# The first head's values are loaded behind the scores of its first query tile

## The chip, the core and the metric

The kernel runs on one core of a Trainium2 chip. The core has a matrix engine (PE, with its own path for loading weights, PEld), a vector engine (DVE), an activation engine (ACT), a general engine (POOL) and a queue engine (SP) that here issues every DMA. Times are microseconds (us) on the device. The metric is the time of one execution; the time before is the median of three runs.

## The reference

One layer of a streaming encoder with two branches. It handles a prompt of 2048 new frames and a sample of 64 frames of running streams. All of it is float32 and the kernel must return eight tensors (two outputs, keys, values and retention states). In short:

```python
h = rmsnorm(x, norm_g) @ w_in                  # 1024 -> 6144 columns
qa, ka, va, za, qb, kb, vb, zb, ga, gb = split(h)
# branch A: 4 heads, each with two 64-wide halves c = 0, 1 of q and k, values 128 wide
s = einsum('bqhcd,bkhcd->bhcqk', q, k) * 64 ** -0.5 - slope * |q_pos - k_pos|
s = where(k_pos // 64 <= q_pos // 64, s, -inf)
p = softmax(s)
a = p[:, :, 0] - lam * p[:, :, 1]
out_a = einsum('bhqk,bkhe->bqhe', a, v)        # then a norm per head
# branch B: retention, chunks of 64, state carried from chunk to chunk
y = x + (sig(ga) * (out_a * silu(za) @ w_o_diff) + sig(gb) * (out_b * silu(zb) @ w_o_ret)) @ w_out
```

## The kernel before

**Splitting.** A float32 product is made of products of high and low parts: every operand `w` is split by a cast on ACT (`wh`) and a subtraction on DVE or POOL (`wl`), and PE does `wh*xh`, `wh*xl` and `wl*xh`. Keys, queries and values are kept in DRAM as two such parts (`kT`, `qT`, `vN`, each a list of two).

**Stages.** Three generators run side by side. `w_stream` makes the input projection: an opening part, blocks done directly (L1137 is the matmul line of those) or by one level of Strassen's scheme (L989), and last `quad` (L1544), which makes the remaining gate columns in seven passes with names `t2, b11, b21, t1, t3, t4, b22`; every pass forms sums of the inputs' blocks and has matmuls on L1564. Its results are added up by DVE on L1584; the fifth pass, `t3`, needs two such additions for each group of matmuls. `z_stream` does the attention of the sample, then that of the prompt (`attn_head`, by half of the prompt, head and query tile `p`), with retention and norms between, then prepares the output stage (`out_prep`). In it the output weights are loaded and split (`load_wo`, L2470 the cast on ACT, L2477 the subtraction on DVE, L2473 that on POOL) and the gated branch results are formed (L2615, L2626). `out_stream` makes the output products.

**One query tile of the prompt attention.** `qk_block` issues, for each of two blocks of 128 queries and both halves c, the score matmuls (L1878 and L1879: high and low parts of `q`) into a bank named `mm`, `s` or `tp`, and a DVE reduction on L1887 that adds the position table (`dnear`, `dfar`) and keeps the minimum. `softmax` exponentiates on ACT (L1918) and combines both halves. `at_pv` transposes the result on PE (L1990, bank `at`), splits it (cast `ath` on ACT, L2004; `atl` on DVE, L2006), and multiplies it with the values (L1968, L1969, L1970, bank `pv`); `a_e` is a small row of sums that L2015 adds. It does not begin until both score blocks are done and the values' load is issued:

```python
yield lambda: pair["n"] == 2 and hd["tv"] is not None
arows, vs = pair["rows"], hd["vs"]
yield max(pair["t"], hd["tv"])
```

**The loads.** `h_loader` runs `load_head` for each head: four K loads (per half of the prompt), then two V loads of 512 KB (`vN[0]`, `vN[1]`). For the first head of all (`self.far` is false) the loads of the first two query tiles and of the table `dfar` stand between K and V. `self.ntile` counts the query tiles whose scores are out; `h_loader` waits for 3 of them before the second head.

**What sets the order.** The order of every engine is written when the program is built. `loop` is a planner: it holds a list of generators with priorities, and keeps a model clock for PE, ACT, DVE, POOL and DMA (`self.pe` and so on). It always runs the first generator, by priority, whose wake time or condition is met. `P`, `A`, `V`, `G`, `ld` and `st` advance the clocks by modelled costs. So a change in when one condition is met can give another order to everything planned later. PE, ACT and DVE run the order as written; each waits at its next instruction until what that needs is done. All DMAs are issued by SP in order (`ld` on L280, `st` on L285) and go round eight semaphores (DMAHW0 to DMAHW7 in the lists below), so that each DMA's issue also waits until the eighth one before it has landed. Buffers that matter here: `thi` and `tlo` (parts of the values on their way to `vN`) have one and two, `ath` and `atl` two each, V four, q two; of PSUM banks there are two `mm`, two `s`, two `at`, one `pv`, one `tp`.

Of the kernel before, what the change touches and what calls it, by code (L numbers as in the profile page):

```python
# [172 lines left out]
class Hybrid:  # L173
# [1595 lines left out]
    def load_head(self, half, h):  # L1769
        ap = self.ap  # L1770
        nu = half + 1
        ks = [[None] * nu for _ in range(2)]
        vs = [[None] * nu for _ in range(2)]
        tk = tv = 0
        for u in range(nu):
            usl = slice(1024 * u, 1024 * u + 1024)
            for c in range(2):
                yield from self.take("K")
                k = self.sb(ap, [128, 1024], "K", dt=F32R)
                for j in range(2):  # L1780
                    o = 64 * (j ^ c)
                    tk = self.ld(k[o:o + 64].bitcast(F32), self.kT[j][h, 64 * c:64 * c + 64, usl], 1 << 18)
                ks[c][u] = k
        hd = {"ks": ks, "vs": vs, "tk": tk, "tv": None}
        if self.far:
            self.heads.append(hd)
        else:
            self.far = True
            yield from self.load_q(0, 0)
            yield self.pe + 3000  # L1790
            yield from self.load_q(0, 1)
            yield self.pe + 2000
            self.ld(self.dfar, self.i["c_dfar"], 1 << 19)
            self.heads.append(hd)
        for u in range(nu):
            usl = slice(1024 * u, 1024 * u + 1024)
            for j in range(2):
                yield from self.take("V")
                v = self.sb(ap, [128, 8, 128], "V", dt=F32R)
                tv = self.ld(v.bitcast(F32), self.vN[j][usl, 128 * h:128 * h + 128]  # L1800
                             .rearrange("(t p) e -> p t e", p=128), 1 << 19)
                vs[j][u] = v
        hd["tv"] = tv
# [1399 lines left out]
```

## Time and profile before

| what | value |
|---|---|
| median of three runs | 1887.12 us (1886.89 to 1887.62) |
| the profiled execution: its time, its span | 1887.63 us, 1885.9 us |
| PE, DVE, ACT, POOL busy | 99%, 71%, 52%, 36% of the span |
| granted PE clock | 1.00 |
| matmuls (PE), transfers on SP's queue | 11090 instructions, 61.7% of 16 DMA engines |
| prompt attention's first score matmul (L1878) | 604.5 us |
| `quad`, first to last addition on L1584 | 1454.8 to 1532.4 us |

The profile counts an engine as busy from an instruction's start to its modelled end. Matmuls overlap, so a matmul's cost on PE is the distance from its start to the next one's start. An entry `[1.31 <-DMA q<-qT]` says that the engine stood idle for 1.31 us before the instruction and that the load of `q` ended that.

### The profile page before, as it was taken

The numbers are of one execution on the slowest core, as the hardware profiler recorded it, in microseconds if no ns is written. First come the engines' busy times: TensorE is split into PE (matmuls) and PEld (weight loads), VectorE is DVE, ScalarE is ACT, GpSimd is POOL, SyncE is SP. The second block draws the span as 40 slices with busy tenths as digits, with TensorE's granted clock in tenths as the row PEclk, the third lists the DMA queues.
The fourth block names the chain that finished last, engine by engine and source line by source line (L and its number), as shares of the span: only waits on it lengthen the run. The fifth ranks groups of instructions, "written<-read, shape, count | busy, mean of one in ns | idle before, by whom it ended". The sixth has DMA issues, their size and how long they took to land.

```text
span 1885.9 us, 33029 instructions
## 1 busy us (share of the span) xinstructions
PE 1867.0 (99%) x11090; PEld 1644.9 (87%) x11090; DVE 1330.5 (71%) x3117; ACT 975.9 (52%) x2266; POOL 669.5 (36%) x723
## 2 busy tenths in 40 slices
PE   9999999999999999999999999999999999999999
PEld 7788878888888789888988889899999899998887
DVE  6765857658585677787587777677866969977664
ACT  6444545554434566556465655556666436654221
POOL 2420266555552122022210344243224625512442
PEclk9999999999999999999999999999999999999999
DMA  7664555666867967556423649446437988886452
GB/s 258 209 177 122 162 165 169 177 199 198 243 185 191 254 196 191 154 170 174 139 73 95 178 131 244 120 130 158 115 115 231 284 233 257 271 237 209 165 157 77
DMA packets 402555, 340.07 MB, mean 180 GB/s; under 512 B 85329, under 2 KB 348625, under 8 KB 401362
## 3 DMA queue, kind: packets, MB, share of 16 engines
q1 hardware_dynamic: 402386, 337.97, 61.7%
q8 instruction: 87, 1.43, 0.3%
q14 instruction: 82, 0.67, 0.1%
HBM read 218.27 MB, written 118.75 MB: 179 GB/s over the span
## 4 chain that ended last, share of the span: by engine, by line
PE 89%; DMA 4%; DVE 4%; issue 1%; SPq 1%; ACT 1%; POOL 0%; DVEq 0%; ACTq 0%; POOLq 0%
PE mm L1137 29%; PE mm L989 8%; PE tp L989 4%; PE at L1990 3%; PE s L1879 2%; PE s L1878 2%; PE s L989 2%; PE pv L1970 2%; PE pv L1969 2%; PE pv L1968 2%; PE mm L1564 1%; PE s L2793 1%; PE s L2795 1%; PE s L2794 1%; PE pv L2256 1%
## 5 line engine op out<-in xcount | busy, mean ns | idle before, releaser
L748 POOL TENSOR_TENSOR wl<-ws,wh 128x512 fp32r<-128x512 f32 x102 | 142.5, 1408 | 240.8 <-ACT wh L727 160.2
L1137 PE MATMUL mm<-wh,xh 128*128 128x512 f32 x504 | 203.0, 403 | 0.0
L1137 PE MATMUL mm<-wh,xl 128*128 128x512 f32 x504 | 198.1, 393 | 0.0
L1137 PE MATMUL mm<-wl,xh 128*128 128x512 f32 x504 | 198.0, 393 | 0.1
L1137 PE MATMUL mm<-xh,wh 128*128 128x288 f32 (+2 forms) x544 | 179.8, 330 | 0.0
L1137 PE MATMUL mm<-xh,wl 128*128 128x288 f32 (+2 forms) x544 | 175.5, 323 | 0.0
L1137 PE MATMUL mm<-xl,wh 128*128 128x288 f32 (+2 forms) x544 | 175.5, 323 | 0.0
L1918 ACT ACTIVATE row<-row,a_mx 128x1024 f32<-128x1024 f32 (+7 forms) x144 | 149.8, 1042 | 11.7 <-DVE a_mx L1897 11.7
L2006 DVE TENSOR_TENSOR atl<-at,ath 128x512 fp32r<-128x512 f32 (+1 forms) x144 | 92.6, 658 | 77.8 <-ACT ath L2004 77.6
L2004 ACT CAST ath<-at 128x512 fp32r<-128x512 f32 (+1 forms) x144 | 79.1, 564 | 106.2 <-PE at L1990 105.7
L856 POOL TENSOR_TENSOR wl<-ws,wh 128x256 fp32r<-128x256 f32 x64 | 55.3, 865 | 197.8 <-ACT wh L847 197.6
L1745 POOL TENSOR_TENSOR r_y<-r_y,r_sq 128x256 f32<-128x256 f32 x32 | 29.7, 929 | 236.2 <-DVE r_sq L1742 152.4
L1137 PEld LDWEIGHTS mm<-wh,xl 128*128 128x128 f32 x504 | 94.6, 188 | 21.6
L1137 PEld LDWEIGHTS mm<-wl,xh 128*128 128x128 f32 x504 | 95.0, 188 | 18.4 <-POOL wl L748 0.9
L1137 PEld LDWEIGHTS mm<-wh,xh 128*128 128x128 f32 x504 | 94.9, 188 | 17.8 <-DVE raw L1308 0.2
L1137 PEld LDWEIGHTS mm<-xh,wh 128*128 128x128 f32 x544 | 102.4, 188 | 7.2
L1137 PEld LDWEIGHTS mm<-xl,wh 128*128 128x128 f32 x544 | 102.5, 188 | 6.9
L1137 PEld LDWEIGHTS mm<-xh,wl 128*128 128x128 f32 x544 | 102.3, 188 | 6.6
L1887 DVE CUSTOM_DVE_ANT_0 row<-s,dfar 128x512 f32<-128x512 f32 (+2 forms) x141 | 87.0, 629 | 23.4 <-PE s L1879 16.8
L1940 DVE SCALAR_TENSOR_TENSOR row<-row,a_w 128x1024 f32<-128x1024 f32 (+5 forms) x88 | 97.3, 1111 | 0.0
L727 ACT CAST wh<-ws 128x512 fp32r<-128x512 f32 x111 | 67.7, 619 | 47.9 <-DMA ws<-wsum 13.2
L1878 PE MATMUL s<-K,q 128*128 128x512 f32 (+3 forms) x240 | 90.5, 379 | 1.3 <-DVE a_acc L1887 1.3
(543 smaller groups left out, 6072.4 us busy)
## 6 DMA issues: line engine op xcount, KB each, us to landing
ws<-in_w_in_dram SPq DMA_DIRECT2D x155, 256.0 KB, 3.4
q<-qT SPq DMA_DIRECT2D x128, 128.0 KB, 3.8
K<-kT SPq DMA_DIRECT2D x48, 256.0 KB, 4.6
V<-vN SPq DMA_DIRECT2D x24, 512.0 KB, 5.9
row<-in_x_prompt_dram SPq DMA_DIRECT2D x16, 512.0 KB, 4.5
wz<-in_w_in_dram SPq DMA_DIRECT2D x32, 256.0 KB, 4.3
row<-in_cache_k_T_dram SPq DMA_DIRECT2D x32, 256.0 KB, 3.2
row<-in_cache_v_diff_dram SPq DMA_DIRECT2D x32, 256.0 KB, 3.6
```

Of the source, the lines that this page charges most:

```text
L727: self.nc.scalar.copy(h, st)
L748: eng.tensor_sub(l, st, h.bitcast(F32))
L856: nc.gpsimd.tensor_sub(l[:, cs], src, h[:, cs].bitcast(F32))
L989: nc.tensor.matmul(ps, w[:, c], xs[x][c], start=bool(tag) and c == 0 and i == 0, stop=c == 3 and i == 2, skip_group_check=True)
L1137: nc.tensor.matmul(ps, p, q, start=c == 0 and i == 0, stop=c == KC - 1 and i == 2)
L1878: nc.tensor.matmul(ps, q1s, kk, start=True, stop=False)
L1887: nc.vector.tensor_tensor_reduce(out=row[:, k0:k0 + n], in0=ps, in1=tab, scale=-SLOPES[h], scalar=3.0e38, op0=ALU.add, op1=ALU.min, accum_ ...
L1918: nc.scalar.activation(u, u, AF.Exp, bias=mx, scale=-1.0, accum_out=lp[:, k:k + 1])
L1940: nc.vector.scalar_tensor_tensor(out=u0, in0=u1, scalar=w[:, 0:1], in1=u0, op0=ALU.mult, op1=ALU.add)
L1990: nc.tensor.transpose(at[:, w:w + 128], src, self.ident)
L2004: nc.scalar.copy(ah[:, :w], at[:, :w])
L2006: nc.vector.tensor_sub(al[:, :w], at[:, :w], ah[:, :w].bitcast(F32))
```

## The change

A condition is added to `load_head`, in the branch for the first head of all: after the table load and after the head has been put into the list, the generator waits until one query tile's scores are out, and only then issues the V loads.

```diff
             yield self.pe + 2000
             self.ld(self.dfar, self.i["c_dfar"], 1 << 19)
             self.heads.append(hd)
+            yield lambda: self.ntile >= 1
         for u in range(nu):
             usl = slice(1024 * u, 1024 * u + 1024)
             for j in range(2):
```

Lines behind L1794 are one higher in the changed kernel (L2005 there is L2004 here, L1969 is L1968, L2478 is L2477). The set of instructions is almost the same on every engine: 10790 rows on PE and 1544 on SP in both, and three subtractions of L748 (`wl` of an input weight) go from DVE to POOL. Their order differs from the moved loads on to the end of the attention and into `quad`.

**SP, at the first tile.** In the kernel before, behind the table:

```order
L280 DMA dfar<-in_c_dfar_dram 128x1920 [waits DMAHW4_49]
L280 DMA V<-vN_61 128x8x128 [waits DMAHW5_49]
L280 DMA V<-vN_62 128x8x128 [waits DMAHW6_49]
L285 DMA qbT<-ev 128x256 [waits DMAHW7_49,Activation_49]
L285 DMA gbT<-ev 128x2x256 [waits DMAHW0_49,DVE_49]
L285 DMA qbT<-ev 128x256 [waits DMAHW1_49,Activation_49]
L285 DMA qbT<-ev 128x32 [waits DMAHW2_49,Activation_49]
L285 DMA qbT<-ev 128x256 [waits DMAHW3_49]
L280 DMA q<-qT_57 64x2x256 [waits DMAHW4_49,PE_49]
L280 DMA q<-qT_57 64x2x256 [waits DMAHW5_49]
```

In the changed kernel:

```order
L280 DMA dfar<-in_c_dfar_dram 128x1920 [waits DMAHW4_49]
L285 DMA qbT<-ev 128x256 [waits DMAHW5_49,Activation_49]
L285 DMA gbT<-ev 128x2x256 [waits DMAHW6_49,DVE_49]
L285 DMA qbT<-ev 128x256 [waits DMAHW7_49,Activation_49]
L285 DMA qbT<-ev 128x32 [waits DMAHW0_49,Activation_49]
L285 DMA qbT<-ev 128x256 [waits DMAHW1_49]
L280 DMA V<-vN_61 128x8x128 [waits DMAHW2_49]
L280 DMA V<-vN_62 128x8x128 [waits DMAHW3_49]
L280 DMA q<-qT_57 64x2x256 [waits DMAHW4_49,PE_49]
L280 DMA q<-qT_57 64x2x256 [waits DMAHW5_49]
```

Both V loads go behind five stores (of `qbT` and `gbT`, results of the projection) and stand right ahead of the first load of the next `q`.

**PE, at the second tile's scores.** Before, where `tp`, `s` on L1878 and L1879 are the second tile's scores, `mm` on L1137 the projection, and `pv` the first tile's product with V:

```order
L1878 MATMUL tp<-K,q 128x256
L1879 MATMUL tp<-K,q 128x256
L1878 MATMUL s<-K,q 128x384
L1879 MATMUL s<-K,q 128x384
L1878 MATMUL s<-K,q 128x256
L1879 MATMUL s<-K,q 128x256
L1137 MATMUL mm<-wh,xh_120 128x512
L1137 MATMUL mm<-wl,xh_120 128x512
L1137 MATMUL mm<-wh,xl_121 128x512
L1968 MATMUL pv<-ath,V 128x256
L1969 MATMUL pv<-ath,V 128x256
L1970 MATMUL pv<-atl,V 128x256
```

Changed:

```order
L1137 MATMUL mm<-wh,xh_120 128x512
L1137 MATMUL mm<-wl,xh_120 128x512
L1137 MATMUL mm<-wh,xl_121 128x512
L1137 MATMUL mm<-wh,xh_120 128x512
L1137 MATMUL mm<-wl,xh_120 128x512
L1137 MATMUL mm<-wh,xl_121 128x512
L1969 MATMUL pv<-ath,V 128x256
L1970 MATMUL pv<-ath,V 128x256
L1971 MATMUL pv<-atl,V 128x256
L1969 MATMUL pv<-ath,V 128x128
L1970 MATMUL pv<-ath,V 128x128
L1971 MATMUL pv<-atl,V 128x128
```

The first tile's products with V now come behind six matmuls of the projection and ahead of the second tile's scores, which follow behind the `a_e` row and three more matmuls of the projection.

**ACT, some 25 us later.** `r_o`, `r_y`, `r_sq` and `r_hi` belong to the norms of retention and of the projection, `thi` and `raw` to values that are stored. Before:

```order
L1703 ACTIVATE r_sq<-r_o 128x256
L1705 ACTIVATE r_hi<-r_o 128x256
L2004 CAST ath<-at 128x512
L1384 CAST thi<-mm 128x512
L1386 COPY raw<-mm 128x512
L2004 CAST ath<-at 128x512
L1729 ACTIVATE r_y<-tp 128x256
L1730 ACTIVATE r_y<-r_y 128x256
L1731 ACTIVATE r_sq<-r_y 128x256
L2004 CAST ath<-at 128x384
```

Changed:

```order
L1703 ACTIVATE r_sq<-r_o 128x256
L1705 ACTIVATE r_hi<-r_o 128x256
L1384 CAST thi<-mm 128x512
L1386 COPY raw<-mm 128x512
L1729 ACTIVATE r_y<-tp 128x256
L1730 ACTIVATE r_y<-r_y 128x256
L1731 ACTIVATE r_sq<-r_y 128x256
L2005 CAST ath<-at 128x512 x2
L2005 CAST ath<-at 128x384
```

The first cast of `at` went behind `thi`, `raw` and the three norm steps, and the three casts of `at` now stand together.

**DVE, in the fifth pass of `quad`.** `u` and `ev` on L1584 are the additions that empty PSUM banks, `xl` the low part of a sum of inputs for a later pass, `w_o_diffl` and `w_o_retl` those of the output weights. Before:

```order
L2477 TENSOR_TENSOR w_o_retl_16953<-wst,w_o_reth_16952 128x2x256
L1584 TENSOR_TENSOR u_16726<-at,u_16726 128x256
L1584 TENSOR_TENSOR u_16727<-at,u_16727 128x288
L748 TENSOR_TENSOR wl<-ws,wh 128x512
L1584 TENSOR_TENSOR u_16726<-mm,u_16726 128x256
L2477 TENSOR_TENSOR w_o_diffl_16951<-wst,w_o_diffh_16950 128x2x256
L1584 TENSOR_TENSOR u_16727<-mm,u_16727 128x288
L2477 TENSOR_TENSOR w_o_retl_16955<-wst,w_o_reth_16954 128x2x256
L1584 TENSOR_TENSOR u_16726<-s,u_16726 128x256
L1584 TENSOR_TENSOR ev<-s,u_16726 128x256
L1584 TENSOR_TENSOR u_16727<-s,u_16727 128x288
L1584 TENSOR_TENSOR ev<-s,u_16727 128x288
```

Changed, at the same count of rows:

```order
L1584 TENSOR_TENSOR u_16576<-at,u_16576 128x288
L2478 TENSOR_TENSOR w_o_diffl_17152<-wst,w_o_diffh_17151 128x2x256
L1529 TENSOR_TENSOR xl_123<-xraw,xh_122 128x544
L1584 TENSOR_TENSOR u_16575<-at,u_16575 128x256
L1584 TENSOR_TENSOR ev<-at,u_16576 128x288
L2478 TENSOR_TENSOR w_o_retl_17154<-wst,w_o_reth_17153 128x2x256
L1529 TENSOR_TENSOR xl_123<-xraw,xh_122 128x544
L1584 TENSOR_TENSOR u_16576<-mm,u_16576 128x288
L2478 TENSOR_TENSOR w_o_retl_17156<-wst,w_o_reth_17155 128x2x256
L1584 TENSOR_TENSOR ev<-at,u_16575 128x256
L1584 TENSOR_TENSOR u_16575<-mm,u_16575 128x256
L2478 TENSOR_TENSOR w_o_diffl_17150<-wst,w_o_diffh_17149 128x2x256
```

The subtractions for the output weights came between additions in both; more of them, and more of `xl`, stand between the additions of this pass in the changed order.

## The prediction

> **What bounds the kernel now.** I read the page's head first, then the matrix engine's waits over the whole run, then its timeline at the places that the change touches, with the DMA queue's beside it, and last the stretches of `quad`.
>
> ```profile
> span 1885.9 us, 33029 instructions
> PE 1867.0 (99%) x11090; PEld 1644.9 (87%) x11090; DVE 1330.5 (71%) x3117; ACT 975.9 (52%) x2266; POOL 669.5 (36%) x723
> ```
>
> PE bounds the whole run, and the change neither adds nor takes a matmul. So it can only move the time by PE's waits: those it takes away, and those the new order makes. The waits put down to one cause, largest first:
>
> ```profile
> PE mm L1564 <- DVE ev L1584: 2.1, 1, 2.1
> ...
> PE s L1564 <- DVE xl L1529: 1.6, 1, 1.6
> PE tp L1878 <- DMA q<-qT: 1.3, 1, 1.3
> PE s L1878 <- DVE a_acc L1887: 1.3, 1, 1.3
> PE pv L1968 <- ACT ath L2004: 1.2, 1, 1.2
> ...
> PE s L1564 <- DVE u L1584: 0.9, 1, 0.9
> ```
>
> Three of these belong to `quad` (L1564), 4.6 us together; the others are single events in the attention.
>
> **The change, first tile: what it may remove.** The second tile's scores wait for their `q`:
>
> ```profile
> 615.96 0.29 PE L1137 MATMUL mm<-xl,wh 128*128 128x288 f32 x1
> 616.09 0.29 PE L1137 MATMUL mm<-xh,wl 128*128 128x288 f32 x1
> 617.68 0.36 PE L1878 MATMUL tp<-K,q 128*128 128x256 f32 x1 [1.31 <-DMA q<-qT]
> 618.39 0.36 PE L1879 MATMUL tp<-K,q 128*128 128x256 f32 x1 [0.35 <-DMA q<-qT]
> ...
> 619.18 0.40 PE L1137 MATMUL mm<-wh,xh 128*128 128x512 f32 x1
> 619.42 0.40 PE L1137 MATMUL mm<-wl,xh 128*128 128x512 f32 x1
> ...
> 619.88 0.28 PE L1968 MATMUL pv<-ath,V 128*128 128x256 f32 x1
> 620.00 0.28 PE L1969 MATMUL pv<-ath,V 128*128 128x256 f32 x1
> ...
> 620.66 0.42 PE L1878 MATMUL tp<-K,q 128*128 128x384 f32 x1
> ```
>
> From start to start a 128x288 matmul takes 0.13 us (616.09-615.96), a 128x512 one 0.24, a 128x256 one 0.12. The step from 616.09 took 1.59, 1.46 too long, that from 617.68 took 0.71, 0.59 too long: 2.05 us lost. In the new order six 128x512 matmuls come first (6 x 0.24, so PE wants V at 616.22+1.44 = 617.7), then the pv block with its a_e row (620.66-619.88 = 0.78) and three more 128x512 (0.72): PE wants the `q` at 619.2. Does the queue deliver both?
>
> ```profile
> 605.41 0.34 SPq L280 DMA_DIRECT2D dfar<-in_c_dfar_dram  x1
> 606.31 1.00 SPq L280 DMA_DIRECT2D V<-vN  x2
> 607.41 2.60 SPq L285 DMA_DIRECT2D qbT<-ev  x1
> 610.13 0.36 SPq L285 DMA_DIRECT2D gbT<-ev  x1
> 610.60 1.67 SPq L285 DMA_DIRECT2D qbT<-ev  x3
> 612.37 3.52 SPq L280 DMA_DIRECT2D q<-qT  x4
> ```
>
> The last of these q loads was issued before 615.9 and the stall ended at 618.4, so `q` is there by the new time if it is issued no more than 0.8 us later; V stands ahead of it, but V's issue (1.00) was ahead of it already. Two prices for V's issue: the five stores move up by V's 1.00 and the first of them, which took 2.60 right behind V, takes the 0.36 of the next one, so V goes out at 612.37-1.00-2.60+0.36 = 609.1; or the stores gain nothing, and V goes out at 612.4.
>
> ```profile
> DMA to landing us min/median/max: 5.6/6.3/6.9
> ...
> DMA to landing us min/median/max: 3.8/5.9/10.4
> ```
>
> The first row is V's in the stretch 600 to 616 us, the second all 24 V loads of the run. Issued at 609.1 V lands by 616.0, 1.7 ahead of 617.7. At the other end 612.4+6.9 = 619.3 is 1.6 late. So this term lies between -2.05 and -2.05+1.6 = -0.4. I take -2.05: the next store, from the same `ev` tiles but not right behind V, took 0.36.
>
> [...]
>
> **The second place: a wait that takes the place of the one removed.** Some 20 us later PE waits for casts of `at`:
>
> ```profile
> 640.99 0.38 PE L1968 MATMUL pv<-ath,V 128*128 128x256 f32 x1 [1.21 <-ACT ath L2004]
> ...
> 641.82 0.39 PE L1970 MATMUL pv<-atl,V 128*128 128x256 f32 x1 [0.33 <-DVE atl L2006]
> ```
>
> The cast that it waits for stands behind `thi`, and that behind the store of the last `thi` (one buffer):
>
> ```profile
> 639.37 0.58 ACT L1384 CAST thi<-mm 128x512 fp32r<-128x512 f32 x1 [2.78 <-DMA vN<-thi]
> ...
> 640.33 0.60 ACT L2004 CAST ath<-at 128x512 fp32r<-128x512 f32 x1
> 640.80 0.42 ACT L1729 ACTIVATE r_y<-tp 128x256 f32<-128x256 f32 x1
> ...
> 642.02 0.46 ACT L2004 CAST ath<-at 128x384 fp32r<-128x384 f32 x1
> ```
>
> ```profile
> 635.34 0.54 SPq L280 DMA_DIRECT2D ws<-in_w_in_dram  x1
> 635.98 0.41 SPq L285 DMA_DIRECT2D vN<-thi  x1
> ```
>
> In the new order `thi`, `raw`, `r_y`, `r_y` and `r_sq` all stand ahead of the casts. From `thi` to the cast was 0.96 (`thi` and `raw`); three norm steps add 1.22 (642.02-640.80). From the cast's start to PE's was 0.66. The `ws` issue in front of the store went ahead among the K loads, which lets the store out 0.64 earlier (635.98-635.34). So pv starts at 639.37-0.64+0.96+1.22+0.66 = 641.57, which is 0.58 later than before. By then PE has issued nine more 128x512 matmuls (9 x 0.24 = 2.16), three 128x128 transposes less (0.06 each, half of a 128x256) and six pv matmuls less (0.12 each): 1.23 us of work that is ahead. The balance of both places is 0.58-1.23 = -0.65; so this one costs +1.4 of the 2.05. Its bounds: all of the old wait gone (-1.21-0.33 = -1.5), or the store not earlier (+1.4+0.64 = +2.0).
>
> **The third place: the splits of the output weights fall into `quad`.** The planner ran more of the projection early, so fewer of its matmuls are left for later: by the order of the two kernels the last pv of the attention comes behind one group of `quad` before, behind twelve and a half now (828 and 690 matmuls of L1564 follow it). What waits for the end of the attention, above all the splits of the output weights on DVE, slides into the fifth pass, in which DVE has the most to do:
>
> ```profile
> 1482.00:1498.00 16.00, 14.04 (x108) 13.69 (x108) 16.00 (x24) 9.09 (x16) 13.86 (x9) 1.00 1.11 342
> 1498.00:1514.00 16.00, 13.95 (x109) 13.65 (x108) 14.94 (x26) 6.49 (x11) 9.92 (x7) 1.00 1.06 277
> ...
> L2477 DVE TENSOR_TENSOR w_o_diffl<-wst,w_o_diffh x5: 677/1435/1462, 1445.4 to 1489.0; 128x512 fp32r<-128x512 f32 x5
> ...
> L1529 DVE TENSOR_TENSOR xl<-xraw,xh x24: 707/1102/1854, 1425.3 to 1514.7; 128x544 fp32r<-128x544 f32 x24
> ...
> L2669 PE MATMUL s<-ogh,w_o_diffh x64: 279/283/289, 1532.2 to 1712.5; 128*128 128x264 f32 x64
> ```
>
> Columns of the first two rows: PE, PEld, DVE, ACT and POOL busy; of the others: shortest, median and longest in ns, first and last start. DVE is busy 16.00 of 16.00 us while PE is at 14.04: here DVE sets the pace, and each more row on it between additions delays PE. Counted in the two orders, between the 20th and 50th addition on L1584 stand 20 other rows before and 25 now (L1529 8 and 10, L2477 5 and 7, L2626 1 and 4, L748 3 and 1, L2615 3 each); between the 50th and 60th there are two fewer. Net three more rows at 1.10 us (the median of L1529, the commonest of them): +3.3. Bounds: nothing, if DVE's lead before this stretch takes them (five fewer stand between the 10th and 20th addition), or less than nothing if the waits of `quad` go (a rival below); above, all five at the 1.435 of L2477, +7.2.
>
> [...]
>
> What comes with it at no cost: three subtractions of L748 go from DVE to POOL (36% busy). The output weights come later by what the attention's end slides in PE's work, 138 matmuls x 0.13 = 18 us; the last DVE split started at 1489.0 and the first output matmul at 1532.2, so 43 us of cover hide it, and it would cost only beyond that. The store and load issues are the same number; nothing else on SP waits for V.
>
> **The sum.** -2.05 + 1.4 + 3.3 = +2.65 us. The profiled execution took 1887.63, 0.5 above the median of the three runs, so I put the sum on the median: 1887.12 + 2.65 = 1889.8. A measurement can tell about 0.2%, 3.8 us, from no change: faster is under 1883.3, slower over 1890.9.
>
> **The rivals.**
> *DVE pays in full in the fifth pass.* All five rows at 1.435 and nothing given back: -0.65 + 7.2 = +6.55, 1893.7. For it: 16.00 of 16.00 busy. Against: fewer rows just ahead and behind. It decides (slower) from a third term of 4.4.
> *`quad` absorbs the rows.* Third term 0: 1886.5. For it: five rows fewer stand between the 10th and the 20th addition, so DVE could enter this stretch further ahead, and in the next one it has 1.06 of 16 us free. Against: it had no gap in the stretch before, so what it is behind stays.
> *`quad`'s waits go (the other side).* Two more of the `xl` rows are done by the 50th addition, so the later passes' inputs are ready sooner; if that and the new spacing of additions take away the three L1564 waits, 4.6, the sum is -0.65-4.6 = -5.25: 1881.9. It decides from a third term of -3.2. Against it: the same DVE has more, not less, to do there.
> *V comes too late.* With the longest landing of the run, 10.4, from 609.1, V lands at 619.5, 1.8 behind PE's wish; PE works in order, so three projection matmuls and the second tile's scores stand behind it, and what waits for those. +2.65+1.8 = +4.45: 1891.6. For it: nothing but that one row. Against: all V loads of that stretch landed within 6.9.
>
> **How the numbers follow.** The sum as worked out 0.40, DVE in full 0.22, absorbed 0.20, `quad`'s waits gone 0.12, V too late 0.06. Any other single wait of the attention can come or go with a new order; the largest after those above is the 1.3 of a_acc, so each case has about 1.5 on either side. Then a quarter of the first case is beyond 1890.9. Faster: 0.12. Slower: 0.10+0.22+0.06 = 0.38. Within: 0.30+0.20 = 0.50. The likeliest is the sum, 1889.8. The range goes from the third rival, 1881.9, to the first with its 1.5, 1895.2; it leaves out half of the 0.12, and about 0.04 above.
>
> **What would show it.** Right: in the new profile no wait for `q` near 618, a wait of 2 to 3 us for `ath` near 641, and L1564's waits for DVE together about 8 in place of 4.6. Wrong, step by step: a wait of L1968 for V at 617 to 620; `thi` not waiting for its store; L1564's waits at or below 4.6. The prediction as a whole would fail if a place far from these three held a new wait of several us, since the order differs everywhere between them.

## The result: slower by half a per cent

The changed kernel takes 1897.27 us (median of 4 runs, 1895.86 to 1900.04), the kernel before 1887.37 us (1886.89 to 1887.69) beside it: a ratio of 1.0054, 95% interval 1.0042 to 1.0066, or 9.9 us. The profiled execution has a span of 1894.5 us against 1885.9, 8.6 more, so nearly all of the loss can be found in its trace. This is outside the predicted range (1881.9 to 1895.2).

PE still bounds the run, with the same 11090 matmuls. Its waits in the changed kernel (the view of PE's waits; total us, times, longest; line numbers are one higher behind L1794, and by 2 to 14 in the experiments):

```profile
PE pv L1969 <- ACT ath L2005: 3.8, 1, 3.8
PE at L1564 <- DVE ev L1584: 3.5, 2, 3.0
PE s L1564 <- DVE ev L1584: 2.2, 1, 2.2
PE mm L1137 <- POOL wl L748: 2.0, 2, 1.1
PE mm L1137 <- ACT wh L727: 1.8, 1, 1.8
PE mm L1564 <- DVE ev L1584: 1.7, 1, 1.7
```

The wait for `q` near 618 is gone and no wait for V is in the list. The wait for `ath` is three times as long. Two rows, `wl` and `wh`, were not there at all. And the waits of `quad` (L1564) sum to 7.4 in place of 4.6.

The stretches in which the two traces differ, first of before, then of the changed kernel (columns: length; busy time of PE, PEld, DVE, ACT and POOL, each with its count; granted clock; DMA share; GB/s):

```profile
600.00:612.00 12.00, 11.19 (x80) 10.64 (x79) 4.77 (x26) 4.68 (x16) 0.00 (x0) 1.00 1.11 276
612.00:636.00 24.00, 22.34 (x135) 19.61 (x134) 15.19 (x49) 12.68 (x30) 6.28 (x5) 1.00 0.95 235
636.00:646.00 10.00, 8.46 (x51) 7.12 (x50) 5.09 (x14) 4.60 (x10) 0.74 (x1) 1.00 0.96 309
...
800.00:830.00 30.00, 29.92 (x165) 25.07 (x164) 24.92 (x74) 18.75 (x47) 11.45 (x9) 1.00 0.53 157
...
1450.00:1484.00 34.00, 32.91 (x260) 32.48 (x258) 28.02 (x42) 20.19 (x36) 15.18 (x11) 1.00 0.90 264
1484.00:1534.00 50.00, 46.57 (x365) 46.09 (x366) 39.36 (x68) 17.70 (x30) 24.47 (x16) 1.00 0.97 267
```

```profile
600.00:612.00 12.00, 11.85 (x85) 11.39 (x85) 6.04 (x30) 6.05 (x20) 0.00 (x0) 1.00 1.11 301
612.00:636.00 24.00, 23.87 (x136) 20.39 (x135) 15.00 (x44) 11.62 (x27) 6.23 (x5) 1.00 0.98 226
636.00:646.00 10.00, 6.17 (x28) 5.14 (x28) 3.56 (x7) 3.63 (x8) 0.72 (x1) 0.83 0.92 302
...
800.00:830.00 30.00, 25.70 (x127) 20.35 (x126) 26.34 (x74) 17.73 (x46) 13.23 (x10) 0.94 0.86 241
...
1450.00:1484.00 34.00, 34.00 (x273) 34.00 (x272) 22.23 (x36) 17.38 (x34) 18.12 (x13) 1.00 0.82 243
1484.00:1534.00 50.00, 42.65 (x333) 41.72 (x332) 43.36 (x69) 23.78 (x43) 29.72 (x20) 1.00 0.96 279
```

PE's idle time is the length less its busy time. From 600 to 636 it falls from 2.47 to 0.28 us: a gain of 2.2. From 636 to 646 it rises by 2.3, from 800 to 830 by 4.2, and from 1450 to 1534 (`quad`) by 2.8. Two of these rows also have a clock under 1: 0.83 of 10 us and 0.94 of 30 us, work of 1.7 and 1.8 us that was not done. The sum is -2.2+2.3+1.7+4.2+1.8+2.8 = +10.6. Between 830 and 1450 PE idles 0.3 less, and ahead of 600, where both kernels have the same order, the two executions differ by 1.5 by chance (the first score matmul starts at 604.5 and at 603.0): together +8.8, against the span's +8.6. (In the kernel before the additions on L1584 begin at 1438.1 us; 1454.8 is the first of them that goes into `ev`.)

The clock's part of this sum, 3.5 us, is counted against an execution of the kernel before whose clock is 1.00 throughout. Most are not like that: its 56 runs beside the experiments have a mean clock of 0.9985 on average, the changed kernel's four runs 0.9968. That difference is about 3 us of work at the full clock, so the size fits; on which places it falls in the executions that were not profiled is not shown.

### The profile page after: what moved, and what is told of

It reads as the page before. It is cut to its first block, busy times and chain, and to the rows that moved or that the text cites. A ratio compares the mean times of both kernels' runs of the same rounds, so it can differ in the third digit from the quotient of the medians.

```text
span 1894.5 us, 33041 instructions
## 1 busy us (share of the span) xinstructions
PE 1870.6 (99%) x11090; PEld 1647.0 (87%) x11090; DVE 1339.8 (71%) x3114; ACT 972.8 (51%) x2266; POOL 679.4 (36%) x726
## 4 chain that ended last, share of the span: by engine, by line
PE 90%; DVE 4%; DMA 3%; issue 1%; ACT 1%; SPq 1%; POOL 0%; DVEq 0%; ACTq 0%; POOLq 0%
PE mm L1137 30%; PE mm L989 8%; PE tp L989 4%; PE at L1991 3%; PE s L1879 2%; PE s L1880 2%; PE s L989 2%; PE mm L1564 2%; PE pv L1971 2%; PE pv L1970 2%; PE pv L1969 2%; PE s L2796 1%; PE s L2795 1%; PE s L2794 1%; DMA V<-vN 1%
## 5 line engine op out<-in xcount | busy, mean ns | idle before, releaser
L748 POOL TENSOR_TENSOR wl<-ws,wh 128x512 fp32r<-128x512 f32 x105 | 148.1, 1421 | 259.8 <-ACT wh L727 217.2
L1137 PE MATMUL mm<-wh,xh 128*128 128x512 f32 x504 | 203.8, 404 | 1.8 <-ACT wh L727 1.8
L1137 PE MATMUL mm<-wl,xh 128*128 128x512 f32 x504 | 198.5, 394 | 2.0 <-POOL wl L748 2.0
L1137 PE MATMUL mm<-wh,xl 128*128 128x512 f32 x504 | 198.7, 394 | 0.0
L1137 PE MATMUL mm<-xh,wh 128*128 128x288 f32 (+2 forms) x544 | 179.3, 330 | 0.0
L1137 PE MATMUL mm<-xh,wl 128*128 128x288 f32 (+2 forms) x544 | 175.6, 323 | 0.0
L1137 PE MATMUL mm<-xl,wh 128*128 128x288 f32 (+2 forms) x544 | 175.6, 323 | 0.0
L2005 ACT CAST ath<-at 128x512 fp32r<-128x512 f32 (+1 forms) x144 | 79.1, 564 | 115.8 <-PE at L1991 112.1
L1137 PEld LDWEIGHTS mm<-wh,xl 128*128 128x128 f32 x504 | 94.9, 188 | 21.6
L1137 PEld LDWEIGHTS mm<-wl,xh 128*128 128x128 f32 x504 | 95.3, 189 | 20.0 <-POOL wl L748 2.7
L1137 PEld LDWEIGHTS mm<-wh,xh 128*128 128x128 f32 x504 | 94.9, 188 | 19.8 <-ACT wh L727 2.0
L1137 PEld LDWEIGHTS mm<-xl,wh 128*128 128x128 f32 x544 | 102.5, 188 | 6.8
L1137 PEld LDWEIGHTS mm<-xh,wh 128*128 128x128 f32 x544 | 102.4, 188 | 6.8
L1137 PEld LDWEIGHTS mm<-xh,wl 128*128 128x128 f32 x544 | 102.3, 188 | 6.7
L1941 DVE SCALAR_TENSOR_TENSOR row<-row,a_w 128x1024 f32<-128x1024 f32 (+5 forms) x88 | 103.5, 1186 | 0.0
L1879 PE MATMUL s<-K,q 128*128 128x512 f32 (+3 forms) x241 | 91.1, 380 | 0.0
```

The costliest lines, as they stand in the source:

```text
L748: eng.tensor_sub(l, st, h.bitcast(F32))
L1137: nc.tensor.matmul(ps, p, q, start=c == 0 and i == 0, stop=c == KC - 1 and i == 2)
L1879: nc.tensor.matmul(ps, q1s, kk, start=True, stop=False)
L1941: nc.vector.scalar_tensor_tensor(out=u0, in0=u1, scalar=w[:, 0:1], in1=u0, op0=ALU.mult, op1=ALU.add)
L2005: nc.scalar.copy(ah[:, :w], at[:, :w])
```

## The experiments

**Is it the late V, or the new order?** The change does two things: it issues two loads later, and by that it makes the planner write another order for every engine. Two kernels take these apart. In the first the planner is told of the loads where it was, but they are issued where the changed kernel issues them; in the order of the instructions only these two rows on SP differ from before.

```diff
-                tv = self.ld(v.bitcast(F32), self.vN[j][usl, 128 * h:128 * h + 128]
-                             .rearrange("(t p) e -> p t e", p=128), 1 << 19)
+                src = self.vN[j][usl, 128 * h:128 * h + 128].rearrange("(t p) e -> p t e", p=128)
+                if half == h == 0:
+                    self.dma = max(self.dma, self.pe) + (1 << 19) / 300.0
+                    tv = self.dma + DMA_LAT
+                    self.held.append((v.bitcast(F32), src))
...
             self.ntile += 1
+            for v, src in self.held:
+                self.nc.sync.dma_start(v, src)
+            self.held = []
```

> Both V loads of the first head are issued where the changed kernel issues them, behind the five stores, but every engine keeps the order of the kernel before. Theory 'the new order costs it, not the late V': no loss; the stores no longer wait behind V, the next q is issued earlier and the 2.05 us stall near 618 shrinks or goes, 1885 to 1887.5 us. Rival 'V is late': most of the ten us come, 1892 to 1897.

Measured: ratio 1.0002 (0.9993 to 1.0011), 1886.79 us beside 1886.69. The late V alone costs nothing that can be measured. But it gains nothing either. PE's waits near the place:

```profile
PE tp L1886 <- DMA q<-qT: 2.4, 1, 2.4
...
PE tp L1887 <- DMA q<-qT: 0.4, 1, 0.4
```

The wait for `q` stayed (2.8 us, against 1.66 before), although SP issued `q` at 607.4 and not at 612.4: PE, too, was there earlier (its last matmul ahead of the wait began at 612.84, not 616.09; 2.6 of these 3.25 us are the difference of the two executions, whose first score matmuls start at 601.9 and 604.5), and from SP's first issue to PE's start the `q` loads took 8.1 us in place of 5.3. The two V loads now go out right ahead of them; that V held them up is likely, but not shown.

The second kernel is the counterpart: the changed kernel with its order on every engine, but the two loads issued where before has them.

```diff
+            early = []
+            for j in range(2):
+                early.append(self.sb(ap, [128, 8, 128], "V", dt=F32R))
+                self.nc.sync.dma_start(early[j].bitcast(F32), self.vN[j][0:1024, 0:128]
+                                       .rearrange("(t p) e -> p t e", p=128))
             yield lambda: self.ntile >= 1
```

> The counterpart: the order of the changed kernel on every engine, but both V loads issued ahead of the five stores, where the kernel before has them. Theory 'order': as the changed kernel, 1895 to 1900 us, with the stalls near 641, 816 to 822 and in quad all there. Rival 'late V': back to 1887 to 1889.

Measured: ratio 1.0051 (1.0037 to 1.0064). The whole loss is there with V as early as before. Its waits have the same rows:

```profile
PE pv L1979 <- ACT ath L2015: 5.1, 1, 5.1
PE at L1564 <- DVE ev L1584: 4.2, 2, 3.3
PE mm L1137 <- POOL wl L748: 1.9, 2, 1.1
PE mm L1137 <- ACT wh L727: 1.8, 1, 1.8
PE mm L1564 <- DVE ev L1584: 1.7, 1, 1.7
```

So the order is the cause; the two loads' place, within 0.1%, is not. It also has no wait for `q` near 618, so that gain belongs to the order too: the first tile's products with V come ahead of the second tile's scores.

**The two places in the attention.** In the changed kernel PE at the first of them, with what the clock did there:

```profile
640.94 0.58 PE L1969 MATMUL pv<-ath,V 128*128 128x256 f32 x1 [3.83 <-ACT ath L2005]
...
642.47 0.41 PE L1971 MATMUL pv<-atl,V 128*128 128x256 f32 x1
...
644.37 0.28 PE L1971 MATMUL pv<-atl,V 128*128 128x256 f32 x1
```

```profile
641.00:642.00 1.00, 1.00 (x3) 0.78 (x4) 1.00 (x2) 0.37 (x1) 0.00 (x0) 0.50 1.09 287
642.00:643.00 1.00, 1.00 (x6) 1.00 (x6) 0.83 (x3) 0.00 (x0) 0.00 (x0) 0.50 0.88 287
...
644.00:645.00 1.00, 1.00 (x7) 0.91 (x7) 0.93 (x2) 0.04 (x1) 0.00 (x0) 0.84 0.99 276
```

The granted clock is 0.50 for some 3.5 us behind the wait, and a 128x256 matmul takes 0.41 in place of 0.28. The cast came late because `thi` on ACT (638.15 us) had waited for the store of the last `thi`, which SP issued at 634.41 behind eight loads of `q`:

```profile
638.15 0.58 ACT L1384 CAST thi<-mm 128x512 fp32r<-128x512 f32 x1 [8.67 <-DMA vN<-thi]
```

```profile
624.75 9.56 SPq L280 DMA_DIRECT2D q<-qT  x8
634.41 0.54 SPq L285 DMA_DIRECT2D vN<-thi  x1
```

The edit is a table: the transfer with the number on the left is held back until the one on the right has been issued.

```diff
+HOLD = {500: 506, 501: 506, 502: 506, 503: 506}
...
+    def issue(self, dst, src):
+        n = self.nissue
+        self.nissue += 1
+        if n in HOLD:
+            self.later.append((HOLD[n], dst, src))
+            return
+        self.nc.sync.dma_start(dst, src)
+        while self.later and self.later[0][0] <= n:
+            self.nc.sync.dma_start(*self.later.pop(0)[1:])
```

> The changed kernel, with the store of the values' high part (vN<-thi) and its two neighbours ahead of the second group of four q loads near 632 us; one later load of the retention (row<-vbN) falls behind about twenty other transfers as well. Theory 'a 4 us wait costs twice, once as a wait and once as half clock after it': the store goes out about 3 us earlier, the 3.99 us stall near 641 shrinks to 1 or less and the half clock behind it goes (1.7 us), so 4 to 5.5 us less than the changed kernel beside it. Rival 'only the wait itself counts': 2.5 to 3.5 less, and a half clock that stays. Rival 'the stall moves on': within 1 us of the changed kernel.

Measured: 1893.86 us, ratio 1.0031 (1.0019 to 1.0043). Each kernel taken against the kernel before beside it, that is 4.3 us under the changed kernel by the ratios (1.0054) and 2.7 by the medians. The wait fell from 3.8 to 1.8:

```profile
PE pv L1983 <- ACT ath L2019: 1.8, 1, 1.8
```

```profile
640.00:642.00 2.00, 2.00 (x13) 2.00 (x14) 1.55 (x4) 0.48 (x1) 0.73 (x1) 0.70 0.41 154
642.00:644.00 2.00, 2.00 (x7) 1.61 (x6) 0.49 (x2) 0.00 (x0) 0.00 (x0) 0.50 0.26 72
```

So the time does not choose between the first reading (4 to 5.5) and the first rival (2.5 to 3.5): the two intervals overlap. The trace is the rival's: the wait lost 2.0 us, and the half clock stayed, behind a wait of only 1.8. But this differs by execution. Three of the six runs have a mean clock of 0.999 and took 1892.0 to 1894.0 us; the profiled one is of the other three (0.996 and 0.997, 1893.8 to 1895.5). And in the kernel with both edits, below, the same wait of 1.7 us, at 638.57, left the clock at 1.00.

The second place is where the changed kernel has waits that before has not. Around it, in the changed kernel, PE and ACT, and then SP:

```profile
816.54 0.50 PE L1137 MATMUL mm<-wl,xh 128*128 128x512 f32 x1 [1.08 <-POOL wl L748]
...
819.85 0.62 ACT L727 CAST wh<-ws 128x512 fp32r<-128x512 f32 x1 [3.14 <-DMA ws<-in_w_in_dram]
...
820.52 0.50 PE L1137 MATMUL mm<-wh,xh 128*128 128x512 f32 x1 [1.83 <-ACT wh L727]
...
821.94 0.80 PE L1137 MATMUL mm<-wl,xh 128*128 128x512 f32 x1 [0.92 <-POOL wl L748]
```

```profile
812.53 2.59 SPq L280 DMA_DIRECT2D q<-qT  x4
...
815.22 1.02 SPq L280 DMA_DIRECT2D ws<-in_w_in_dram  x2
```

The weights that PE wants next are issued behind four `q` loads, land at about 819.8, and then pass the cast and the subtraction. The edit moves the two `ws` loads ahead of the four: `HOLD = {655: 661, 656: 661, 657: 661, 658: 661}`.

> The changed kernel, with two weight loads (ws) ahead of the four q loads near 813 us. Theory: the waits for wh and wl at 820 and 822 (2.00 and 1.19 us) go, and with them the half clock behind them (1.7 us): 3 to 5 us less than the changed kernel beside it. Rival 'the waits move on': within 1 us of it.

Measured: 1893.05 us, ratio 1.0031 (1.0019 to 1.0043), 4.3 us under the changed kernel by the ratios and 3.5 by the medians: in the theory's range. The clock from 800 to 830 is 1.00. PE still idles 2.6 us there, in place of 4.3, since a wait of 0.9 for `q` came up and, of the rows of `wh` and `wl`, one is left:

```profile
PE mm L1151 <- POOL wl L762: 1.1, 1, 1.1
```

Both edits in one kernel:

> The changed kernel with both edits of the two runs before this one (store first near 632 us, weight loads first near 813). If the two places lose independently, their gains add: 1893.86 and 1893.05 are 3.4 and 4.2 us below the changed kernel's 1897.27, so 1889.6 (1888.5 to 1891). Rival 'what is gained at one place is waited for at the next': 1893 or more.

Measured: 1890.68 us beside 1888.99, ratio 1.0016 (1.0006 to 1.0026). By the ratios the two places took 0.0038 of the 0.0054, some 7 us of 10, and their gains nearly add (0.0023 each, every ratio to about 0.001). What is left, about 3 us by the ratio and 1.7 by the medians, has the size of the third place, `quad`, but the trace doesn't put it down to that place alone: PE still idles 2.8 us from 800 to 830, the waits of `quad` sum to 5.3 us (4.6 in before), and the clock is 0.50 in `quad` from 1499 to 1505.

**What a long wait costs behind it.** In the kernel before, the one cast that PE waits for at 641 is done seven times over.

```diff
+            for _ in range(6 if self.ncast == 4 else 0):
+                nc.scalar.copy(ah, at)
+            self.ncast += 1
             nc.scalar.copy(ah[:, :w], at[:, :w])
```

> The kernel before, with the cast at 640.33 us done seven times over instead of once (same operands), so that PE's wait there grows by 6 x 0.48 = 2.9 us to about 4.3 and nothing else is moved. Theory 'a wait that long costs half clock behind it': +2.9 for the wait and +1.7 for the clock, 1890.5 to 1892, and in the trace half clock for 3 to 4 us behind it. Rival 'only the wait counts': 1889 to 1890 and clock 1.00 there.

Measured: 1893.58 us beside 1888.99, ratio 1.0023 (1.0014 to 1.0031), 4.3 us. The wait became 5.4 and not 4.3 us, so the time alone doesn't tell the readings apart (4.2 for the wait alone, 5.9 with the clock). The trace does show the clock:

```profile
644.38 0.58 PE L1968 MATMUL pv<-ath,V 128*128 128x256 f32 x1 [5.43 <-ACT ath L2007]
```

```profile
645.00:646.00 1.00, 1.00 (x5) 0.90 (x5) 0.14 (x2) 0.84 (x3) 0.00 (x0) 0.50 1.10 317
646.00:647.00 1.00, 1.00 (x5) 1.00 (x5) 0.97 (x3) 0.00 (x0) 0.00 (x0) 0.50 0.31 115
647.00:648.00 1.00, 1.00 (x4) 0.77 (x4) 0.77 (x4) 0.00 (x0) 0.70 (x1) 0.68 0.00 0
```

**`quad`: are DVE's rows what PE waits for?** First all subtractions of the output weights went from DVE to POOL, in the changed kernel.

```diff
-            nc.vector.tensor_sub(l, s, h.bitcast(F32))
+            nc.gpsimd.tensor_sub(l, s, h.bitcast(F32))
```

> The changed kernel, with all subtractions of the output weights' splits (L2478) issued on POOL, with the planner's model unchanged, so that PE and ACT keep their order and DVE only loses 18 rows. Theory 'DVE's extra rows make quad's waits': the L1564 waits for DVE, 8.0 us in the changed kernel's trace, fall to 3 or less, 4 to 6 us in all: 1891.5 to 1893.5. Rival 'POOL or the order of the other rows sets them': the waits stay above 6 and the time within 2 us of 1897.3. A late output weight would show as a wait of L2670 to L2672.

Measured: 1905.37 us, ratio 1.0088 (1.0072 to 1.0103). It failed as a test, since it made a new cause: two subtractions of `xl` on DVE took 10.94 us (before: 0.71 to 1.85 us each) while POOL ran without a gap from 1499.7 to 1524.8, and PE waited 9.9 us behind them.

```profile
1515.10 10.94 DVE L1529 TENSOR_TENSOR xl<-xraw,xh 128x544 fp32r<-128x544 f32 x2
```

```profile
1514.92 1.30 POOL L2478 TENSOR_TENSOR w_o_diffl<-wst,w_o_diffh 128x512 fp32r<-128x512 f32 x1
...
1523.56 1.27 POOL L748 TENSOR_TENSOR wl<-ws,wh 128x512 fp32r<-128x512 f32 x1
```

Then DVE was rid of the same 18 rows without giving POOL any: a copy on ACT writes the low parts, which are then not the remainder, in the changed kernel and in before.

```diff
-            nc.vector.tensor_sub(l, s, h.bitcast(F32))
+            nc.scalar.copy(l, s)
```

> The changed kernel with the low parts of the output weights made by a copy on ACT in place of DVE's subtraction (they are then the whole weight and not the remainder, so the output products are not the reference's): DVE loses 18 rows, POOL gains none, PE keeps its order. Theory 'DVE's extra rows make the waits of quad': the L1564 waits, 8.0 us in the changed kernel's trace, fall to 4 or less, and the time to 3 to 6 us under the changed kernel's distance to before (+9.9), so +4 to +7. Rival 'these waits come from elsewhere (stores of ev, sums on L1529)': +9 to +11.

Measured: ratio 1.0048 (1.0036 to 1.0060), 9.1 us over before by the ratio and 8.5 by the medians: at the rival's lower end, not in the theory's range. DVE had time to spare (7.29 of 16 us busy from 1498 to 1514), and PE waited all the same:

```profile
PE at L1564 <- DVE ev L1584: 3.6, 2, 3.2
PE mm L1564 <- DVE ev L1584: 2.1, 1, 2.1
...
PE s L1564 <- DVE ev L1584: 0.8, 1, 0.8
```

```profile
1513.51 0.42 DVE L1584 TENSOR_TENSOR ev<-at,u 128x256 f32<-128x256 f32 x1 [7.99 <-DMA gbT<-ev]
```

6.5 us of waits are left of 7.4. The two longest now stand later, at 1514 and 1518: DVE itself idles 7.99 us for a buffer `ev` whose store has not landed. In the changed kernel the same addition starts at almost the same time, with the rows on DVE ahead of it in place of most of the wait:

```profile
1513.27 0.43 DVE L1584 TENSOR_TENSOR ev<-at,u 128x256 f32<-128x256 f32 x1 [0.84 <-DMA gbT<-ev]
```

So DVE's rows delay the additions ahead of this one, but what they cost there is waited for here without them.

> The same on the kernel before: the L1564 waits, 5.0 us there, with DVE rid of the same 18 rows. Theory: 3 to 5 us less than before, since five of these rows stand in its fifth pass too. If the rows matter only in the changed order: within 1 us of before.

Measured: ratio 0.9997 (0.9989 to 1.0005): nothing here either, with 4.3 us of L1564 waits in place of 4.6. So in both orders the rows on DVE are not the only limit of this stage. In the changed order the store of `ev` stands behind them; in the old one, from 1455 to 1535 and without the rows, DVE waits 8.4 us in all for casts of ACT (`xh`), and 1.0 and 1.1 us for such stores. How the changed kernel's 2.8 us divide between the rows and the stores is open.

**Is this order bad, or is any new one?** Three kernels have a new order with no load moved by hand. Two change one number of the planner's, by an eighth either way (`FIRSTQ`, 4000 to 4500 and to 3500), one a condition (`ntile >= 3` to `>= 2` in `h_loader`).

> The kernel before with one number of the planner changed, FIRSTQ from 4000 to 4500 (the modelled delay of the first q loads); no load and no wait is put elsewhere by hand, but PE, DVE and ACT get another order from there on, as they do by the change. Theory 'the order of before is a tuned draw and any new draw loses some us at places far from the edit': 1890 to 1900. Rival 'the loss belongs to what this change does': 1884 to 1889.

> The kernel before with FIRSTQ at 3500 instead of 4000: a new order again, in the other direction, no load moved by hand. Theory 'before is a tuned draw, a new one loses at places far from the edit': 1890 to 1903, with waits at other places than the changed kernel's. Rival 'only later loads lose': 1884 to 1889.

> The kernel before with the second head's loads allowed after two query tiles in place of three: a third new order, by a condition of the same kind as the change's but for another load. Theory 'tuned draw': 1890 to 1903. Rival: 1884 to 1889.

Measured: 1.0063 (1.0050 to 1.0075), 1.0059 (1.0044 to 1.0073) and 1.0085 (1.0069 to 1.0100): by the ratios 11 to 16 us slower, all three (9.5 to 13.8 by the medians). The waits are in part at other places. But the largest wait of the kernel with 4500 is the changed kernel's first place again, at 646, by the same chain: casts behind `thi`, `raw` and three norm steps, and `thi` waiting 8.3 us for a store issued behind eight loads of `q`.

```profile
PE pv L1968 <- ACT ath L2004: 3.7, 1, 3.7
```

The kernel with the other condition waits most in `quad`, for `xl` (5.9 us). The one with 3500 waits in `quad`, the output stage and the retention:

```profile
PE tp L1719 <- DVE u L1584: 2.2, 1, 2.2
PE s L2669 <- DVE ev L1584: 1.9, 1, 1.9
...
PE s L2335 <- DMA row<-qbT: 1.6, 1, 1.6
```

None of the new orders beat the kernel before. All four edits act at the loads of the first two heads; one that acts elsewhere was not tried, so it is open whether any new order loses, or one that stirs up this stretch.

## Why the prediction was wrong

The direction of the sum was right (+2.65 us), its size was not (+9.9), and the range, up to 1895.2, ended 2 us short.

*The first tile.* Predicted -2.05, measured -2.2. V went out at 607.08, or at 608.6 with the 1.5 us that this execution is ahead, beside the predicted 609.1, and no wait for it is in the list, so "V comes too late" fell. The reason given held: the new order puts matmuls ahead of the second tile's scores, so PE wants `q` later. The old order waits for `q` even when it is issued 5 us earlier, as the first experiment shows; the new one does not wait even with V early and `q` issued at 611.87, about as late as before. The close number is in part luck. Only 1.5 of the 2.2 lie at this place (612 to 636); the other 0.7 come from a wait of 0.79 for the first tile's `q`, at 605.5 in before, which the prediction did not count.

*The second place.* Predicted: pv at 641.57 after a wait of 2 to 3 us, +1.4. Measured: pv at 640.94 after 3.83, +2.3 of idle time and +1.7 of work lost at half clock. The wait was 0.8 to 1.8 us longer than predicted. One step of it did not come: the store of `thi` was to go out 0.64 us earlier, but counted from the first score matmul it goes out at 31.4 us in the changed kernel (634.41-603.0) and at 31.5 in before (635.98-604.5). And the term lacked the clock behind the wait. (By the prediction's own figures the work that is ahead is 2.16-0.18-0.72 = 1.26 us, not 1.23; the difference does not matter here.)

In the changed kernel the clock was 0.50 for some 3.5 us behind this wait of 3.83. In one run it followed a wait of 1.8 us (the one with the store first, above). Length alone does not decide it in these runs, since the changed kernel's wait of 3.0 us in `quad` passed with the clock at 1.00; what does is not shown.

*The third place.* Predicted +3.3, measured +2.8 more idle time from 1450 to 1534. The size holds, by luck in part; the mechanism, more rows on a full DVE, is not all of it: without the rows 6.5 of the 7.4 us of waits are still there, because the stores of `ev` are waited for.

*The step that failed* is in "How the numbers follow": "Any other single wait of the attention can come or go with a new order; the largest after those above is the 1.3 of a_acc, so each case has about 1.5 on either side". The trace of before can't price the waits of an order that it doesn't have. The changed one idled 4.2 us more from 800 to 830, above all in new waits at 816 to 822, and with the half clock behind them lost 6.0: most of the miss of 7.3 (9.9 less 2.65). The last sentence ahead of the forecast named this as what would make it fail, but no chance was given to it, and the three other redraws, at +11 to +16 by the ratios, suggest that it should have had the largest.

## What to carry to other kernels

In a kernel whose planned order keeps PE busy for 99% of the time, a change that makes the planner write a new order is first of all a new draw: four draws of four lost 10 to 16 us by the ratios, whatever the edit was for. To try such an edit, hold the order fixed and move only the transfer; whether another new order would bring a gain is then a question of its own, which no run here answers. And allow for the clock behind a wait of PE: in these traces it cost 1.7 to 2.0 us of work beside a single wait of 1.8 to 5.4 us in the attention, and nothing behind one of 1.7 there and one of 3.0 in `quad`.

## What the runs showed of the hardware

The clock: behind waits of 1.8 to 5.4 us PE's granted clock was 0.50 for 3 to 4 us in several traces, 1.7 to 2.0 us of work each time (the 2.0 behind the 5.1 us of the kernel with V early, where the clock was 0.50 from 640, before that wait had ended); behind one of 3.0 and one of 1.7 it stayed at 1.00. It is not the same in each execution: the changed kernel's four runs have mean clocks of 0.995 to 0.998, the slowest run with the lowest. Nor does all of this work become time. The first experiment's profiled execution has half clock from 617 to 620 and a mean clock of 0.998, and it takes no longer than before (1886.79 us). And of the 56 runs of the kernel before, the eight with a mean clock of 1.000 are on average only 1.3 us below, each beside its own group's mean, the 26 with 0.998, where 0.002 of the span is 3.8 us.

DVE and POOL: a subtraction of `xl` (128x544) takes 0.71 us at its shortest, 1.10 in the median and 1.85 at its longest in the kernel before; with all of the output weights' subtractions on POOL, two of them took 10.94 us while POOL ran one instruction after the other. The trace shows the lengths, not who held what.
